# First layer of a hybrid decoder: the RMSNorm root moved from the input to the products

## The chip, the cores and the metric

The kernel runs on one core of one Trainium2 chip. The metric is the device time of one execution in microseconds; the time given for the kernel is the median of three runs. TensorE (PE) multiplies matrices, VectorE (DVE), ScalarE (ACT) and GpSimd (POOL) work on elements, and SyncE (SP) issues the DMAs here.

## The reference

Four layers run over 1040 tokens (16 meta tokens and 1024 of the sequence) of width 1024: sliding-window attention (a), an mLSTM (b), an HGRN2 (c) and attention again. Each layer normalizes the stream, runs its branch and adds the result. What concerns the change is the first attention layer:

```python
def rmsnorm(x, g):
    y = xf * lax.rsqrt(jnp.mean(xf * xf, axis=-1, keepdims=True) + EPS)
    return (y * g.astype(jnp.float32)).astype(x.dtype)
...
q, k, v, z = _split(u @ w_in, (A_W, A_KVW, A_KVW, A_W))
q = rope(rmsnorm(q.reshape(bsz, lp, A_HEADS, A_HD), q_gain), pos)
k = rope(rmsnorm(k.reshape(bsz, lp, A_KV, A_HD), k_gain), pos)
v = v.reshape(bsz, lp, A_KV, A_HD)
o = sliding_window_attention(q, k, v, sinks, valid)
return (o * jax.nn.silu(z.astype(jnp.float32))).astype(u.dtype) @ w_out
```

with `u = rmsnorm(h, norm_gain[i])` in front. The root of the mean square, r, is one number for a token, so (r x g) W = r ((x g) W): it can be applied to the products as well. q and k are normalized once more per head; there r cancels except in the small EPS: with q' = q / r, the root of mean(q'^2) + EPS / r^2 gives the same normalized q.

## The kernel before

Everything is stored with features on the 128 partitions and tokens along the free axis: `x` is 128 x 8 x 1040 fp32. Tokens come in three chunks of 400, 384 and 256 columns (`CHUNKS`). fp32 products are made of three: each operand is split into a high part (a cast to the fp32r type, on ScalarE) and a low part (the remainder, on VectorE; `split`, L194 and L195), and high x high, high x low and low x high add up in PSUM. The normalized input is kept that way in `uh` and `ul`.

`proj` makes one projection tile: 128 output features, for each chunk four steps of two k-slices, six products to a step, 24 to a chunk (L228). `weights` loads a tile's weights in two halves of 256 KB into the `raw` buffers (RAWS = 2) and splits them; a step's third entry, `pre`, does this ahead of time (LOOKAHEAD). An `evac` function takes the finished chunk out of PSUM.

The order of TensorE's work is written by hand: `steps` is a list of [cost, function, pre], and functions such as `later`, `spread` and `weave` insert steps at due times counted in cost. The other engines' instructions, and SyncE's DMAs, are ordered by the Tile scheduler. Each engine runs its own instructions in order. PSUM has eight banks, all shared. Work buffers: `tmp()` gives one of six (TMPS) 128 x 404 buffers, `row()` one of eight 128 x 1040.

The norm (`Norm`) of the first layer runs like this for chunk 0, before any product: square each of eight k-slices on ScalarE (L352), add them in pairs on VectorE (L356), sum over the partitions by a matmul with ones (L364), take Ln and Exp for the root (L338, L339), multiply x by gain and root on VectorE (L386), split the result into `uh` and `ul`. Chunks 1 and 2 follow between the products; their adds are on GpSimd (`squares`, `stat`, `units`, placed by `FIRST`).

The head of layer 0 is three tiles over three chunks: k0, qa and qb (in this order in each chunk; in chunk 0 the first halves of k0 and qa stand together). A q or k chunk is evacuated by ScalarE twice, times the gain (L492) and squared (L493); four small DMAs swap halves for the rotary embedding (L496); later `stat` (k, a matmul with a mask and Ln, Exp) or `stat_q` (q, per token and head, L516 to L519) makes the second norm's root, `rope` rotates, and `k_split` or `q_split` (L444 to L464) splits. Then the attention mixers run, woven step by step with the rest of the projections: v tiles, q tiles, the gate tiles z (`gate_proj`: a sigmoid of five instructions and two products on VectorE, L400 to L412), k1, and the output projections (L322, added to x at L325).

Of the kernel before, what the change touches and what calls it, by code (L numbers as in the profile page):

```python
# [46 lines left out]
PARTS = 4  # L47
FIRST = (0.2, 0.8, 0.85), (0.2, 0.75, 0.8)
# [63 lines left out]
def hybrid_kernel(ctx: ExitStack, tc: tile.TileContext, ins, out, layers=(0, 1, 2, 3)):  # L112
# [47 lines left out]
    eps = cpool.tile([P, 1], F32, name="eps")  # L160
    v.memset(eps, EPS)
    one = cpool.tile([P, 1], F32, name="one")
# [7 lines left out]
    def load_x(n):  # L170
        c0, cn = CHUNKS[n]
        for k in range(KT):
            sp.dma_start(x[:, k, c0 : c0 + cn], ins["xT"][k, :, c0 : c0 + cn])

    load_x(0)
# [35 lines left out]
    def proj(src, evac, chunks=CHUNKS):  # L211
# [129 lines left out]
    class Norm:  # L341
        def __init__(self, i, row=None):
            self.i, self.row, self.acc, self.ps = i, row, {}, {}

        def sq(self, m, n, c0, cn, size=KT):
            if m % size:
                q = tmp()[:, :cn]
            elif self.row is not None and n:
                q = self.row[:, c0 : c0 + cn]
            else:  # L350
                q = (vtile() if n == 2 else tmp())[:, :cn]
            s.activation(q, x[:, m, c0 : c0 + cn], AF.Square)  # L352
            if m % size == 0:
                self.acc[n] = q
            else:
                (v if self.row is None or n == 0 else g).tensor_tensor(self.acc[n], self.acc[n], q, op=ALU.add)  # L356

        def stat(self, n, part=0, parts=1):
            cn = CHUNKS[n][1]

            def fn():
                if part == 0:
                    self.ps[n] = psa()
                pe.matmul(self.ps[n][:, :cn], ones, self.acc[n], start=(part == 0), stop=(part == parts - 1))  # L364
                if part == parts - 1:
                    rstd_from(self.ps[n], self.acc[n], cn, D)

            return [4 * cn * MM, fn, None]

        def squares(self, n, part=0, parts=1):  # L370

            size = KT // parts

            def fn():
                for m in range(part * size, (part + 1) * size):
                    self.sq(m, n, *CHUNKS[n], size)

            return [0.0, fn, None]
# [18 lines left out]

    def sigmoid_from(z, cn):
# [8 lines left out]
    def gate_proj(src, o, chunks=CHUNKS):  # L407
# [6 lines left out]
        return proj(src, evac, chunks)  # L414

    def layer_a(i, j, first, last, fin):
# [69 lines left out]
        def qk_proj(src, gcol, work, fsplit, ch, t=None):  # L486
            late = {}

            def evac(acc, n, c0, cn):
                dst, sq, rot = work(n, c0, cn)  # L490
                late[n] = dst, sq, rot
                s.activation(dst, acc[:, :cn], AF.Identity, scale=R["cons"][:, gcol : gcol + 1])  # L492
                s.activation(sq, acc[:, :cn], AF.Square)  # L493
# [4 lines left out]
            def finish(n, c0, cn):  # L498
                def factors():
# [4 lines left out]
                    late[n] += (R["cs"][1][:, :, c0 - b0 : c0 - b0 + cn],)  # L504

                def stat_q():
# [11 lines left out]
                    s.activation(rq[:, z], st[:, z], AF.Ln, bias=eps, scale=1.0 / 64)  # L518
# [23 lines left out]
            return proj(src, evac, ch), [finish(n, *c) for n, c in enumerate(ch)]  # L542
# [21 lines left out]
        def v_proj(src, jj):  # L564
# [7 lines left out]
            def finish(n, c0, cn):  # L572
                def fn():
# [4 lines left out]
                    for k, b in enumerate(CHUNK_BLOCKS[n]):  # L578
# [7 lines left out]
                        s.copy(parts[:, 0:4:3], src)  # L586
                        v.tensor_tensor(parts[:, 1:3], src, parts[:, 0:4:3].bitcast(F32), op=ALU.subtract)
# [107 lines left out]
        zc = {t: gate_proj(win[12 + t], lambda t=t: R["o", t], chunks) for t in range(8)}  # L695
# [808 lines left out]
```

## Time and profile before

| what | value |
|---|---|
| runs shown | 2623.77, 2625.77, 2625.26 us, median 2625.26 |
| profiled execution, its time | 2624.74 us |
| its span (first to last instruction) | 2623.0 us |
| mean granted TensorE clock | 0.993 |
| VectorE, ScalarE, GpSimd busy | 75%, 64%, 10% of the span |
| DMA | 135.92 MB, mean 52 GB/s |

In a page's groups a line reads: source line, engine, operation, output <- inputs with shapes, count, then busy time and mean ns of one, then the idle time before them and what ended it. A line of the waits reads: who waited, for whom, total us, times, longest. A line of the timeline reads: start, length in us, instruction, count, and in brackets the idle time in front of it. SPq is SyncE's queue, where DMAs are issued; L206 are weight loads.

### The profile page before, as it was taken

The page shows a single profiled execution, that of the slowest core. Times are in us where ns is not written, and L with a number is a line of the kernel's source. Part 1 is how long each engine was busy: PE and PEld are TensorE (multiplying, and loading weights), DVE is VectorE, ACT ScalarE, POOL GpSimd, SP SyncE. Part 2 cuts the span into 40 slices and gives each one's busy share as a digit, 9 for nine tenths or more (in the row PEclk, how much of TensorE's full clock was granted, in tenths as well). Part 3 has the DMA queues.
Part 4 walks back from the last instruction along what each step waited for, and adds up shares of the span by engine and source line. Part 5 has one row for each costly group of instructions (what it writes and reads, how often), then busy time and mean ns, then how long its engine had stood idle before and what let it go on. Part 6 is the DMA issues. An engine that isn't in the chain of part 4 may idle for free. (4 is left out here: it accounts for less than half of the span.)

```text
span 2623.0 us, 54248 instructions
## 1 busy us (share of the span) xinstructions
PE 2565.2 (98%) x20422; PEld 2484.6 (95%) x20422; DVE 1970.6 (75%) x5296; ACT 1665.7 (64%) x4374; POOL 249.8 (10%) x502
## 2 busy tenths in 40 slices
PE   7999999989999999999999999999999999999999
PEld 5999999989999999999999999999999999999999
DVE  6798798784747474747475688989787978887996
ACT  6776767565454545454545657878585857767772
POOL 2221221000000000000000000100000100321330
PEclk9999999999999999999999999999999999999999
DMA  4212111021111111111111101011110112212112
GB/s 129 68 50 84 55 44 48 22 66 49 42 56 41 57 41 56 42 53 45 53 45 49 49 26 50 26 42 34 34 42 30 38 51 86 59 50 84 55 39 79
DMA packets 82583, 135.92 MB, mean 52 GB/s; under 512 B 12033, under 2 KB 35713, under 8 KB 82321
## 3 DMA queue, kind: packets, MB, share of 16 engines
q1 hardware_dynamic: 82320, 132.45, 16.2%
q8 instruction: 161, 2.64, 0.4%
q14 instruction: 102, 0.83, 0.1%
HBM read 117.56 MB, written 4.26 MB: 46 GB/s over the span
## 5 line engine op out<-in xcount | busy, mean ns | idle before, releaser
L228 PE MATMUL pj<-uh,wh 128*128 128x256 f32 (+2 forms) x2688 | 916.4, 341 | 9.6 <-ACT uh L194 9.6
L228 PE MATMUL pj<-ul,wh 128*128 128x256 f32 (+2 forms) x2688 | 867.9, 323 | 2.2 <-DVE ul L195 1.7
L228 PE MATMUL pj<-uh,wl 128*128 128x256 f32 (+2 forms) x2688 | 864.6, 322 | 0.0
L228 PEld LDWEIGHTS pj<-uh,wh 128*128 128x128 f32 x2688 | 510.2, 190 | 26.8 <-ACT uh L194 13.2
L228 PEld LDWEIGHTS pj<-ul,wh 128*128 128x128 f32 x2688 | 510.5, 190 | 11.1 <-DVE ul L195 5.8
L228 PEld LDWEIGHTS pj<-uh,wl 128*128 128x128 f32 x2688 | 510.0, 190 | 0.0
L194 ACT CAST wh<-wr 128x512 fp32r<-128x512 f32 (+1 forms) x338 | 203.2, 613 | 110.9 <-PE pj L322 32.7
L195 DVE TENSOR_TENSOR wl<-wr,wh 128x512 fp32r<-128x512 f32 (+1 forms) x338 | 233.7, 701 | 51.6 <-ACT wh L194 49.3
L325 DVE TENSOR_TENSOR x<-x,pj 128x384 f32<-128x384 f32 (+2 forms) x480 | 234.7, 508 | 35.0 <-PE pj L322 33.7
L322 PE MATMUL pj<-yh,wh 128*128 128x384 f32 (+2 forms) x768 | 253.0, 329 | 8.0 <-DVE x L325 6.2
L322 PE MATMUL pj<-yh,wl 128*128 128x384 f32 (+2 forms) x768 | 245.2, 319 | 0.0
L322 PE MATMUL pj<-yl,wh 128*128 128x384 f32 (+2 forms) x768 | 245.2, 319 | 0.0
L277 PE MATMUL pj<-wh,uh 128*128 128x256 f32 (+1 forms) x768 | 231.9, 302 | 0.0
L277 PE MATMUL pj<-wl,uh 128*128 128x256 f32 (+1 forms) x768 | 216.5, 282 | 0.0
L277 PE MATMUL pj<-wh,ul 128*128 128x256 f32 (+1 forms) x768 | 216.2, 281 | 0.0
L635 POOL TENSOR_TENSOR Sm<-Sm,s 128x512 f32<-128x512 f32 (+2 forms) x136 | 142.1, 1045 | 449.4 <-DVE s L634 434.5
L632 ACT ACTIVATE Sm<-Sm,s 128x257 f32<-128x257 f32 (+2 forms) x272 | 130.9, 482 | 79.5 <-DVE s L629 75.3
L404 ACT ACTIVATE t<-t 128x384 f32<-128x384 f32 (+2 forms) x240 | 117.9, 491 | 87.8 <-DVE t L403 86.0
L403 DVE SCALAR_TENSOR_TENSOR t<-pj,t 128x384 f32<-128x384 f32 (+2 forms) x192 | 98.7, 514 | 80.0 <-ACT t L402 78.1
L322 PEld LDWEIGHTS pj<-yh,wh 128*128 128x128 f32 x768 | 144.2, 188 | 11.7 <-DVE x L325 7.4
L194 ACT CAST yh<-r 128x384 fp32r<-128x384 f32 (+2 forms) x120 | 57.1, 478 | 151.9 <-PE pj L322 139.8
L277 PEld LDWEIGHTS pj<-wh,uh 128*128 128x128 f32 x768 | 144.6, 188 | 2.1
(255 smaller groups left out, 5423.0 us busy)
## 6 DMA issues: line engine op xcount, KB each, us to landing
wr<-in_b_win SPq DMA_DIRECT2D x124, 256.0 KB, 2.8
wr<-in_a_win SPq DMA_DIRECT2D x80, 256.0 KB, 2.9
wr<-in_c_win SPq DMA_DIRECT2D x64, 256.0 KB, 2.8
wr<-in_a_wout SPq DMA_DIRECT2D x32, 256.0 KB, 2.8
wr<-in_b_wout SPq DMA_DIRECT2D x32, 256.0 KB, 2.8
t<-t SPq DMA_DIRECT2D x104, 48.0 KB, 1.9
cs<-in_rope SPq DMA_DIRECT2D x11, 400.0 KB, 3.4
cs<-in_rope SPq DMA_DIRECT2D x11, 384.0 KB, 3.6
```

Source lines behind the costliest of these rows:

```text
L194: s.copy(h, src)
L195: v.tensor_tensor(l, src, h.bitcast(F32), op=ALU.subtract)
L228: pe.matmul(acc[:, :cn], a[:, k, :], b[:, k, c0 : c0 + cn], start=(k == 0 and i == 0), stop=(k == KT - 1 and i == 2))
L277: pe.matmul(acc[:cn, :nc], a[:, k, c0 : c0 + cn], m[:, kk, :], start=(k == 0 and j == 0), stop=(k == KT - 1 and j == 2))
L322: pe.matmul(acc[:, :cn], a[:, k, mc], b, start=(k == 0 and i == 0), stop=(k == 1 and i == 2))
L325: v.tensor_tensor(x[:, m, c0 : c0 + cn], x[:, m, c0 : c0 + cn], acc[:, :cn], op=ALU.add)
L403: v.scalar_tensor_tensor(a[:, :cn], z, 0.0, a[:, :cn], op0=ALU.min, op1=ALU.subtract)
L404: s.activation(a[:, :cn], a[:, :cn], AF.Exp)
L632: s.activation(Sm[:nq, u, : nk + 1], Sm[:nq, u, : nk + 1], AF.Exp, scale=-1.0, bias=st[:nq, u : u + 1], accum_out=den[:nq, u : u + 1])
L635: g.tensor_tensor(Sm[:nq, :, :nk], Sm[:nq, :, :nk], den[:nq].rearrange("p (u c) -> p u c", c=1).to_broadcast([nq, 2, nk]), op=ALU.mult)
```

## The change

In the first layer `uh` and `ul` hold x times the norm's gain, without the root. A new class `Scale` makes the root beside it:

- `unit` makes `uh` with one ScalarE pass from x (the gain as scale) and `ul` with one VectorE pass (x times gain minus `uh`).
- `squares` sums the squares per chunk: ScalarE squares chunks 0 and 1, GpSimd chunk 2, and GpSimd does all adds.
- `sums` makes the root twice: per token on the partitions (`rcol`, and `ecol` = EPS times mean square plus EPS squared) by a product of each block with a column of ones, and along the free axis in `row` by a matmul with ones, Ln and Exp; the row is also written to DRAM.
- `fetch` reads that row back, broadcast to 128 partitions.

The root is applied behind the products: k0's chunks are multiplied by `row`; k1's and the gates' by a fetched row, whose DMA is issued when the second quarter of the chunk's products is (`early`); v's blocks by `rcol` when they are split; q is not multiplied, but its second norm takes `ecol` in place of EPS.

The head's order becomes qa, qb, k0 in each chunk, with the first halves of qa and qb together in chunk 0. qb's work buffers are those of the mixers (`idle`). At the start SyncE is given the gain, the first tile's weights, four slices of x, the second tile's weights, four slices of x, then chunk 1 of x. `Norm` loses what only the first layer used.

```diff
-FIRST = (0.2, 0.8, 0.85), (0.2, 0.75, 0.8)
+FIRST = (0.1, 0.2, 0.9), (1.0, 1.1, 1.9)
+SUMS = 0.8, 1.5, 2.5
...
+                    if part == 1 and early is not None:
+                        early(n, c0, cn)
...
+    class Scale:
...
+        def unit(self, n, k):
...
+            def fn():
+                gain = ngain[:, self.i, k : k + 1]
+                s.activation(uh[:, k, cs], x[:, k, cs], AF.Identity, scale=gain)
+                v.scalar_tensor_tensor(ul[:, k, cs], x[:, k, cs], gain, uh[:, k, cs].bitcast(F32),
+                                       op0=ALU.mult, op1=ALU.subtract)
...
+        def squares(self, n):
...
+                for m in range(KT):
+                    q = tmp()[:, :cn] if m else acc
+                    z = x[:, m, c0 : c0 + cn]
+                    if n < 2:
+                        s.activation(q, z, AF.Square)
+                    else:
+                        g.tensor_tensor(q, z, z, op=ALU.mult)
+                    if m:
+                        g.tensor_tensor(acc, acc, q, op=ALU.add)
...
+        def sums(self, n):
...
+                pc = psa()
+                for k, b in enumerate(bs):
+                    q0 = blk(b)[0] - c0
+                    pe.matmul(pc[:, k : k + 1], acc[:, q0 : q0 + P], ones[:, 0:1], start=True, stop=True)
+                r, e = (z[:, bs[0] : bs[-1] + 1] for z in (self.rcol, self.ecol))
+                s.activation(e, pc[:, : len(bs)], AF.Identity, bias=self.eps2, scale=EPS / D)
+                s.activation(r, pc[:, : len(bs)], AF.Ln, bias=eps, scale=1.0 / D)
+                s.activation(r, r, AF.Exp, scale=-0.5)
+                pr = psa()
+                pe.matmul(pr[:, :cn], ones, acc, start=True, stop=True)
+                rstd_from(pr, acc, cn, D)
+                sp.dma_start(self.dram[c0 : c0 + cn], acc[0:1])
...
+        def fetch(self, dst, c0, cn):
+            sp.dma_start(dst[:, :cn], self.dram[c0 : c0 + cn].partition_broadcast(P))
...
+        def early(n, c0, cn):
+            rs[n] = tmp()
+            scale.fetch(rs[n], c0, cn)
+
         def evac(acc, n, c0, cn):
             cs = slice(c0, c0 + cn)
-            a = sigmoid_from(acc[:, :cn], cn)
-            v.tensor_tensor(a[:, :cn], a[:, :cn], acc[:, :cn], op=ALU.mult)
+            z = acc[:, :cn]
+            if scale is not None:
+                z = rs[n][:, :cn]
+                v.tensor_tensor(z, z, acc[:, :cn], op=ALU.mult)
+            a = sigmoid_from(z, cn)
+            v.tensor_tensor(a[:, :cn], a[:, :cn], z, op=ALU.mult)
             v.tensor_tensor(o()[:, cs], o()[:, cs], a[:, :cn], op=ALU.mult)
...
+                if first and t is None:
+                    v.tensor_tensor(sq, sq if fetched else scale.row[:, c0 : c0 + cn], z, op=ALU.mult)
+                    z = sq
+                s.activation(dst, z, AF.Identity, scale=R["cons"][:, gcol : gcol + 1])
+                s.activation(sq, z, AF.Square)
...
+                        v.scalar_tensor_tensor(rq.rearrange("p (k c) -> p k c", c=2),
+                                               st[:, z].rearrange("p (k c) -> p k c", c=2), 1.0 / 64, e,
+                                               op0=ALU.mult, op1=ALU.add)
+                        s.activation(rq, rq, AF.Ln)
...
+                            s.activation(high, src, AF.Identity, scale=r)
+                            v.scalar_tensor_tensor(parts[:, 1:3], src, r, high.bitcast(F32), op0=ALU.mult, op1=ALU.subtract)
...
+            parts = [tile_of([z[0][n]], [z[1][n]]) for z in ((qa, qb, k0) if first else (k0, qa))]
...
-    for k in range(PARTS):
-        steps += [norm.squares(0, k, PARTS), norm.stat(0, k, PARTS)]
-    steps += [norm.unit(0, k) for k in range(KT)]
+    norm = Scale(layers[0])
+    steps += [norm.unit(0, k) for k in range(KT)] + [norm.squares(0)]
...
+            for n in (2, 1, 0):
+                later(seq, (at(SUMS[n]), norm.sums(n)))
+            for n in (2, 1):
+                t0, t1, t2 = (at(z) for z in FIRST[n - 1])
+                later(seq, *sorted([(t0, norm.squares(n))] + norm.units(n, t1, t2), key=lambda e: e[0]))
...
+    pres = [z for z in steps if z[2] is not None]
+    for z, k0, k1 in ((pres[0], 0, 4), (pres[1], 4, 8)):
+        z[2]()
+        z[2] = None
+        load_x(0, k0, k1)
     load_x(1)
```

More of the change, by code (lines that the diff above doesn't have):

```diff
@@ L693, in mixers @@
             return segs
-        zc = {t: gate_proj(win[12 + t], lambda t=t: R["o", t], chunks) for t in range(8)}
+        zc = {t: gate_proj(win[12 + t], lambda t=t: R["o", t], chunks, scale) for t in range(8)}
         oc = {t: proj_out(wout[t - 1], wout[t], lambda k, t=t: R["o", t - 1 + k], chunks,
@@ L698, in layer_a @@
         kg0, kfin0 = qk_proj(win[0], 1, work_rows(3), k_split(0), CHUNKS)
-        kg1, kfin1 = qk_proj(win[1], 1, tmps, k_split(1), CHUNKS)
+        kg1, kfin1 = qk_proj(win[1], 1, tmps, k_split(1), CHUNKS, fetched=first)
         vg0, vfin0 = v_proj(win[2], 0)
         vg1, vfin1 = v_proj(win[3], 1)
-        qg = {t: qk_proj(win[4 + t], 0, tmps, q_split(t), chunks, t) for t in range(8)}
+        qg = {t: qk_proj(win[4 + t], 0, idle if first and t == 1 else tmps, q_split(t), chunks, t) for t in range(8)}
         def q_pair(p):
@@ L1343, in hybrid_kernel @@
         if i % 3 == 0:
-            head, body, oa, ob = layer_a(i, i // 3, tail is None, i == 3, fin)
+            head, body, oa, ob = layer_a(i, i // 3, tail is None, i == 3, fin, norm if tail is None else None)
         elif i % 3 == 1:
```

135 lines of the change are left out of this document (75 added, 60 removed).

## Prediction

> **What bounds the kernel now.** I read the page's summary first, then the waits of TensorE, then the first 82 us in order of time.
>
> ```profile
> span 2623.0 us, 54248 instructions
> PE 2565.2 (98%) x20422; PEld 2484.6 (95%) x20422; DVE 1970.6 (75%) x5296; ACT 1665.7 (64%) x4374; POOL 249.8 (10%) x502
> PE   7999999989999999999999999999999999999999
> ```
>
> TensorE is busy 98% of the span, and only the first of the 40 slices (65.6 us each) shows a 7. So the question is what the first 82 us lose, and whether anything later loses. TensorE's waits, first in the head (0 to 82 us), then in the rest of the layer up to 450 us:
>
> ```profile
> PE pj L228 <- ACT uh L194: 9.1, 8, 2.9
> ...
> PE pa L364 <- POOL r L356: 2.0, 1, 2.0
> PE pj L228 <- DVE ul L195: 1.7, 4, 0.6
> ```
>
> ```profile
> PE pt L647 <- POOL Sm L635: 2.5, 4, 1.2
> PE pm L621 <- DVE Pl L650: 1.7, 1, 1.7
> PE pt L577 <- ACT t L570: 0.4, 1, 0.4
> ```
>
> In the head every wait is for the normalized input (`uh`, `ul`) or its statistic. Behind the head TensorE waits 4.6 us in three kinds of wait, and 0.5 in two smaller ones, of 369; so there TensorE sets the time, and whatever shortens the head shortens the run by as much.
>
> The start, in order of time:
>
> ```profile
> 0.74 3.71 SPq L173 DMA_DIRECT2D x<-in_xT  x8
> 3.27 1.00 ACT L352 ACTIVATE t<-x 128x400 f32<-128x400 f32 x2 [1.26 <-DMA x<-in_xT]
> 14.06 1.62 ACT L194 CAST uh<-t 128x400 fp32r<-128x400 f32 x3 [0.70 <-DVE t L386]
> 14.64 0.70 PE L228 MATMUL pj<-uh,wh 128*128 128x400 f32 x1 [2.75 <-ACT uh L194]
> ```
>
> The first x lands at 3.27, yet the first product starts at 14.64: squares, sum, root and scaling stand between. How fast products then run, from the stretches of the head (length, TensorE busy and products; granted clock, DMA share, GB/s; the two long stretches without a shape filter):
>
> ```profile
> 14.64:19.92 5.28, 4.96 (x14) 1.00 0.42 142
> 20.17:28.80 8.63, 8.63 (x47) 1.00 0.74 228
> 57.24:60.60 3.36, 3.36 (x18) 1.00 0.24 59
> 78.32:81.35 3.03, 3.03 (x25) 1.00 0.11 30
> 44.00:54.00 10.00, 8.60 (x29) 0.50 0.19 54
> 64.00:78.00 14.00, 12.31 (x47) 0.52 0.16 44
> ```
>
> A product costs 8.63/47 = 0.184 us at 400 columns, 3.36/18 = 0.187 at 384, 3.03/25 = 0.121 at 256. A tile of 24 products per chunk is 24 x 0.492 = 11.8 us, and the head's three tiles (k0, qa, qb) 35.4. The head's last product ends at 81.35. The first stretch runs at 5.28/14 = 0.377 instead of 0.184: 2.7 us lost to a slow start. In 44 to 54 and 64 to 78 the granted clock is 0.50 and 0.52: 10 x 0.50 + 14 x 0.48 = 11.7 us lost.
>
> Small matmuls between them:
>
> ```profile
> 28.80 0.83 PE L525 MATMUL pa<-r,masks 128*128 128x400 f32 x2
> 31.60 0.91 PE L364 MATMUL pa<-r,ones 128*128 128x384 f32 x2 [1.98 <-POOL r L356]
> 33.44 0.95 PE L516 MATMUL pa<-masks,t 128*128 128x2 f32 x8
> 57.00 0.59 PE L364 MATMUL pa<-r,ones 128*128 128x256 f32 x2
> 60.60 0.72 PE L516 MATMUL pa<-masks,t 128*128 128x2 f32 x6
> 82.44 0.50 PE L516 MATMUL pa<-masks,t 128*128 128x2 f32 x4
> ```
>
> k's statistic, about 2.3 for three chunks; q's 2 x (0.95 + 0.72) = 3.3 inside the head; the norm's 1.5 after the start. With the 35.4 that is 42.5. Check: 14.64 + 42.5 + 2.7 + 11.7 + waits after the start (9.1 - 2.75 + 2.0 + 1.7 = 10.1) = 81.6 against 81.35. The head is understood.
>
> **The change part by part.**
>
> *The first product no longer waits for the root.* Only x, ngain, the weights and one ScalarE pass (`uh`) stand before it. SyncE now sends ngain and two weight halves first. At 3.71/8 = 0.46 us an issue, the first x goes out at about 2.1 instead of 0.74.
>
> The rate of transfers in the first 82 us, in slices of 2.05 us:
>
> ```profile
> GB/s 9 261 283 379 375 397 380 367 52 17 306 229 234 164 88 77 33 4 0 4 75 25 0 19 173 43 53 0 67 29 0 0 0 79 21 82 100 18 0 60
> ```
>
> A weight half takes 2.9 us from issue to landing (median of the run):
>
> ```profile
> wr<-in_a_win SPq DMA_DIRECT2D x80, 256.0 KB, 2.9
> ```
>
> From 6 us on 367 to 397 GB/s move, before that 261 to 283. The two halves (524 KB) stand 1.9 us ahead of x at 272: first x at 3.27 + 0.4 for ngain + 1.9 = 5.6, plus a pass of 1.62/3 = 0.54: first product at 6.1 (bounds 5.4 if transfers overlap more, 7.4 if the weight's cast is last). The new pass (a scale read from a column) isn't in the trace; its nearest rows are the square at 3.27 (0.50) and the cast at 14.06 (0.54); I take the cast.
>
> *TensorE's need in the head.* 35.4 for the tiles; k's statistic for two chunks inside the head, 1.6 (k0 now stands last); q's 2 x (0.95 + 0.72 + 0.50) = 4.3; the new `sums` per chunk one full matmul like L364 and one product per block like L516's: (0.91 + 0.95) + (0.9 + 0.72) + (0.59 + 0.50) = 4.5. Sum 45.8. The slow start stays: 2.7.
>
> *The data's pace.* x's first chunk (1.64 MB) and two weight tiles (1.05 MB) take 7.9 us at some 340 GB/s, so all of it is there near 11. Two buffers (RAWS = 2) hold the raw halves of a weight tile, so the second tile's go out only when the first tile's have landed (0.74 + 0.46 + 2.9 = 4.1 for the first half) and are cast and subtracted; if SyncE has issued x's slices meanwhile, they stand behind 1.6 MB. k0's weights come later still: behind x's second chunk it is 4.8 MB in all, 14.1 us + 3.2 = 17.3, plus the cast 17.9, when TensorE wants them at 6.1 + 2.7 + 48 x 0.184 = 17.6. So waits of 0 (weights slip ahead of x) to 7 us (3 at the second tile, 4 at k0 if chunk 2 of x goes first too). I take 2.
>
> *The vector side.* The totals of the first 81.35 us come first below. The old units' multiply by the root goes, 24 instructions; `ul` becomes a multiply and subtract in one. Four adds leave VectorE; the last chunk's squares and all adds are GpSimd's.
>
> ```profile
> sum 81.35, PE 62.56 PEld 52.18 DVE 50.63 ACT 51.22 POOL 13.99; mean PE 12.51 PEld 10.44 DVE 10.13 ACT 10.24 POOL 2.80
> ```
>
> The groups concerned (count, busy and mean ns of one):
>
> ```profile
> L386 DVE SCALAR_TENSOR_TENSOR t<-x,ngain,r 128x384 f32<-128x384 f32 (+1 forms) x16 | 8.4, 546 | 4.3 <-ACT r L339 4.3
> L386 DVE SCALAR_TENSOR_TENSOR t<-x,ngain,t 128x400 f32<-128x400 f32 x8 | 5.4, 720 | 2.2 <-ACT t L339 2.2
> ```
>
> ```profile
> L356 POOL TENSOR_TENSOR r<-r,t 128x384 f32<-128x384 f32 x7 | 7.5, 1069 | 22.8 <-ACT t L352 22.5
> L356 POOL TENSOR_TENSOR r<-r,t 128x256 f32<-128x256 f32 x7 | 5.8, 826 | 17.5 <-ACT t L352 17.0
> ```
>
> VectorE: 50.6 - 13.8 - 2.3 (four adds at 0.57, the price of L464's row below), plus some 3 for k0's row product and q's small sums: 37.5; `ul` lies between that 0.57 and L386's 0.72, so up to 3.4 more. ScalarE: 51.2 less eight squares of 256 columns (0.5 each at 400), plus nine instructions on a few columns: about 50. GpSimd: 7 adds at about 1.1, 7.5, and 15 at 0.826: 27.6, twice what it was. A new head of some 56 us of work has room for VectorE, and ScalarE is 50/56 = 89% full; that will cost some waits. But `uh` and `ul` for chunks 1 and 2 no longer hang on a statistic, so the long waits before `uh`, and with them the half clock, should mostly go. Against 10.1 + 11.7 us before I leave 3.5 (0 to 11).
>
> The head's end: 6.1 + 45.8 + 2.7 + 2 + 3.5 = 60.1, gain 81.35 - 60.1 = 21.2.
>
> *Behind the head.* Each of 24 gate evacuations gets one VectorE product (some 0.55 us, as L464's), 13 us in all, and a 200 KB broadcast fetch on SyncE, issued after the first quarter of its products into a buffer of TMPS; k1's three chunks the same. V's split and q's statistic change form, not count.
>
> ```profile
> 150.00:175.00 25.00, 25.00 (x173) 23.78 (x172) 22.30 (x66) 21.48 (x64) 6.40 (x10) 1.00 0.18 61
> 425.00:450.00 25.00, 25.00 (x162) 24.97 (x161) 18.22 (x36) 16.49 (x37) 0.42 (x1) 1.00 0.28 82
> ```
>
> ```profile
> SPq L206 <- DVE wl L195: 108.8, 27, 25.1
> ```
>
> Where gates run, VectorE is 73 to 89% full and TensorE still does not wait; DMA is at 18 to 28%. So most of the 13 us is covered by TensorE's own products; if that cover were gone it would cost up to 13. In return the bank of PSUM comes free after one instruction instead of six, worth at most the 5.1 us that TensorE waits there. I take a loss of 1.5 (from -3 to +6).
>
> Gain 21.2 - 1.5 = 19.7. The profiled execution took 2624.74, 0.5 below the median 2625.26. Against the median: **2605.6**.
>
> **Two rules that speak against it.** The trace grants 0.50 after a wait of 2.9 us. The Trainium skill ("TensorE: Matmul & The Clock Gate", Part 1, "The HAM clock gate") has the clock fall to half after an idle window of about 3.4 us and come back after one as long of steady work; the trace agrees roughly, with 2.9. By it the waits of the pacing could each drag some 3.4 us at half speed behind them, an estimate of 1.7 us each, 61.8 in place of 60.1.
>
> GpSimd and VectorE disturb each other in the trace:
>
> ```profile
> 24.90 3.31 POOL L356 TENSOR_TENSOR r<-r,t 128x384 f32<-128x384 f32 x3 [3.16 <-ACT t L352]
> 25.11 0.93 DVE L428 TENSOR_SCALAR cons<-cons 128x16 f32<-128x16 f32 x1
> 47.78 0.57 DVE L464 TENSOR_TENSOR qs<-t,qs 64x400 fp32r<-64x400 f32 x1
> 48.58 6.25 POOL L356 TENSOR_TENSOR r<-r,t 128x256 f32<-128x256 f32 x7 [17.03 <-ACT t L352]
> 52.26 1.99 DVE L464 TENSOR_TENSOR qs<-t,qs 64x400 fp32r<-64x400 f32 x2 [3.30 <-ACT qs L463]
> ```
>
> The same subtraction takes 0.57 alone and 1.0 while GpSimd adds; a tiny one takes 0.93. That is the first rival's mechanism. The Trainium skill ("SBUF — State Buffer", "Who interferes with whom") says that a VectorE instruction with two SBUF inputs and a GpSimd one that reads SBUF shut each other out for a whole instruction; the rows agree.
>
> **The rivals.**
>
> *A, VectorE starved by GpSimd.* `ul` is a two-input VectorE instruction and TensorE's second product needs it. With GpSimd busy 27.6 us, some 27 VectorE instructions take 0.4 longer: 11 us, most of it while `ul` of chunks 0 and 1 and the weights' low halves are due. TensorE then waits as before, and half-clock stretches stay. For it: the rows above. Against: VectorE lost 16 us of work. Waits at 11.5 instead of 3.5: gain 11.7, **2613.6**.
>
> *B, slower.* SyncE's queue is in order, and weight loads wait in it for raw buffers: 108.8 us in 27 waits, 4.0 each. A fetch behind one arrives late, the gate's evacuation stands, its PSUM bank stays taken, and TensorE stops. It decides once TensorE loses 21.2/24 = 0.88 us per fetch; at 1.2 us each, 28.8 us go: 2625.3 - 21.2 + 28.8 = **2633**. Against: eight banks, and the fetch has three quarters of a group to arrive.
>
> *C, all stalls gone.* Weights arrive in time and nothing else waits: 6.1 + 45.8 + 2.7 = 54.6, gain 26.7, body even: **2598.5**.
>
> **How the numbers follow.** Forecast 0.60, A 0.19, C 0.13, B 0.08. The forecast's own bounds run from 2600 to 2611; to hold 8 in 10 the range reaches past C's figure and A's: 2597 to 2617. The measurement tells 0.2%, 5.3 us, from no change: A's slow end and B's mild end give 0.04 for no change, B's rest 0.06 for slower, 0.90 for faster.
>
> **What would show it.** First product near 6.1 us; the first vg0 product (now 81.35) near 60; no stretch of ten us at half clock; waits of TensorE for `uh` under 3 us beside short ones for `wh` near 10 and 18. A would show `ul` waits and VectorE instructions of 1.0 us, B waits before gate products or a lengthened 60-to-430 stretch. Wrong would be an unchanged start, or a body longer by over 6 us.

## The result, and the profile after

The changed kernel takes 2635.05 us (median of 8 runs, 2632.55 to 2639.73) against 2626.06 for the kernel before beside it: a ratio on record of 1.0031 with an interval of 1.0020 to 1.0041 (the two medians by themselves give 1.0034). It is slower by 0.3%, where 2605.6 and a gain of 0.75% were forecast. Its profiled execution took 2633.37 with a span of 2631.6, 8.6 us over the span of before.

The page's summary: span, TensorE's busy time, its 40 slices of 65.8 us.

```profile
span 2631.6 us, 54400 instructions
...
PE 2567.6 (98%) x20434; PEld 2492.9 (95%) x20434; DVE 1982.8 (75%) x5323; ACT 1668.8 (63%) x4375; POOL 268.2 (10%) x517
...
PE   7998999989999999999999999999999999999999
```

The first slice still has its 7, and the 8 in the ninth stood there before; new is the 8 in the fourth, 197 to 263 us. The head first. In order of time, TensorE's first product and the first product of the tile vg0 behind the head:

```profile
6.11 0.70 PE L229 MATMUL pj<-uh,wh 128*128 128x400 f32 x1 [6.11 <-ACT uh L398]
...
66.95 0.34 PE L229 MATMUL pj<-uh,wh 128*128 128x400 f32 x1
```

Before, that vg0 product came at 81.35: the head gave 14.4 us. All of it and 8.6 more are lost behind it, 23.0 in all. TensorE's waits in the head (total, times, longest), and two stretches of it (length, then busy time and instructions of PE, PEld, DVE, ACT, POOL; granted clock, DMA share, GB/s):

```profile
PE pj L229 <- ACT uh L398: 6.1, 1, 6.1
PE pj L229 <- ACT wh L193: 4.4, 1, 4.4
PE pa L591 <- ACT t L568: 3.2, 1, 3.2
PE pj L229 <- DVE wl L194: 0.5, 1, 0.5
```

```profile
22.00:28.00 6.00, 5.42 (x15) 4.85 (x16) 6.00 (x6) 4.08 (x9) 5.68 (x5) 0.50 0.38 132
...
33.60:42.00 8.40, 8.35 (x31) 8.33 (x32) 4.12 (x8) 5.44 (x17) 6.26 (x10) 0.50 0.22 55
```

After the start two waits are left, for k0's weights (4.4, and 0.5 for their low half) and for q's statistic (3.2). Behind each the clock is granted at 0.50, for 6 and for 8.4 us, so these two waits cost 8.1 us of standing and (5.42 + 8.35)/2 = 6.9 of half speed.

The waits behind the head, 65 to 450 us:

```profile
PE pa L608 <- ACT t L568: 8.5, 3, 5.0
PE pm L710 <- DVE Pl L739: 4.0, 2, 2.5
PE pt L736 <- POOL Sm L724: 3.6, 4, 1.9
```

The first row is new: L608 is k's statistic, three times, once for each chunk of k1. The kernel before waited 0.2 us in that place. Around it, SyncE's queue, VectorE, ScalarE and TensorE in order of time, from four answers of the timeline:

```profile
238.12 2.42 SPq L571 DMA_DIRECT2D t<-t  x4
240.64 0.53 SPq L446 DMA_DIRECT2D t<-scaled  x1
...
246.44 2.67 SPq L571 DMA_DIRECT2D t<-t  x4
249.21 0.53 SPq L446 DMA_DIRECT2D t<-scaled  x1
...
245.21 0.55 DVE L565 TENSOR_TENSOR t<-t,pj 128x384 f32<-128x384 f32 x1 [4.08 <-DMA t<-scaled]
...
248.62 0.57 DVE L617 TENSOR_TENSOR t<-t,t 128x400 f32<-128x400 f32 x1
...
245.80 0.61 ACT L567 ACTIVATE t<-t,cons 128x384 f32<-128x384 f32 x1 [4.33 <-DVE t L565]
...
239.09 0.94 PE L608 MATMUL pa<-t,masks 128*128 128x400 f32 x2 [2.00 <-ACT t L568]
247.03 0.91 PE L608 MATMUL pa<-t,masks 128*128 128x384 f32 x2 [1.56 <-ACT t L568]
255.07 1.22 PE L608 MATMUL pa<-t,masks 128*128 128x256 f32 x2 [4.95 <-ACT t L568]
```

Read it as a ring. The swaps of one chunk go out at 238.12; only behind them, at 240.64, the fetch of the root for the next chunk; the product with it starts at 245.21, the scaling at 245.80, the statistic at 247.03, the next swaps at 246.44, the next fetch at 249.21. The statistics stand 7.9 and 8.0 us apart, although a chunk's 24 products need 4.4 at most. SyncE stands for 3.8 us before the swaps of 246.44 and hardly at all before the fetch behind them. But the third fetch, at 249.21, goes out just when VectorE's last use of the first chunk's row ends (L617, 248.62 + 0.57 = 249.19); with six work buffers, three to a chunk, this is the buffer that the third chunk's row goes into. From issue to landing, by the list of DMA issues, the fetch is slower than a swap (size of each, median us):

```profile
t<-t SPq DMA_DIRECT2D x36, 50.0 KB, 2.0
t<-scaled SPq DMA_DIRECT2D x9, 200.0 KB, 3.4
t<-scaled SPq DMA_DIRECT2D x9, 192.0 KB, 4.5
```

What the stage lost, in stretches of ten us (columns as above), after and then before:

```profile
240.00:250.00 10.00, 8.44 (x45) 7.76 (x43) 4.94 (x10) 5.19 (x11) 0.00 (x0) 0.83 0.53 148
250.00:260.00 10.00, 5.05 (x15) 4.71 (x15) 4.75 (x9) 5.67 (x12) 0.00 (x0) 0.68 0.51 145
...
sum 40.00, PE 31.43 PEld 29.51 DVE 23.08 ACT 24.55 POOL 1.40; mean PE 7.86 PEld 7.38 DVE 5.77 ACT 6.14 POOL 0.35
```

```profile
sum 40.00, PE 39.33 PEld 37.82 DVE 29.70 ACT 31.30 POOL 4.12; mean PE 9.83 PEld 9.46 DVE 7.43 ACT 7.82 POOL 1.03
```

From 230 to 270 TensorE is busy 7.9 us less than before, and 8.44 x 0.17 + 5.05 x 0.32 = 3.1 us are lost to the clock: 11 us. The ring stands in the one stage where no attention step is woven between a tile's products, so nothing covers it.

### The profile page after: what moved, and what is told of

Read it like the earlier page. It is cut to its first block, busy times and chain, and to the rows that moved or that the text cites. A ratio compares the mean times of both kernels' runs of the same rounds, so it can differ in the third digit from the quotient of the medians.

```text
span 2631.6 us, 54400 instructions
## 1 busy us (share of the span) xinstructions
PE 2567.6 (98%) x20434; PEld 2492.9 (95%) x20434; DVE 1982.8 (75%) x5323; ACT 1668.8 (63%) x4375; POOL 268.2 (10%) x517
## 4 chain that ended last, share of the span: by engine, by line
PE 77%; DVE 11%; ACT 7%; DMA 2%; issue 2%; POOL 1%; SPq 0%; DVEq 0%; ACTq 0%; POOLq 0%
PE pj L229 37%; PE pj L323 15%; PE pj L278 10%; PE po L755 2%; PE pt L736 1%; PE po L998 1%; ACT Sm L721 1%; DVE wl L194 1%; PE pa L1012 1%; PE po L1000 1%; DVE Sm L718 1%; DMA cs<-in_rope 1%; PE pj L274 1%; PE pm L710 1%; PE pm L711 1%
## 5 line engine op out<-in xcount | busy, mean ns | idle before, releaser
L194 DVE TENSOR_TENSOR wl<-wr,wh 128x512 fp32r<-128x512 f32 (+1 forms) x338 | 235.7, 707 | 53.0 <-ACT wh L193 50.3
L721 ACT ACTIVATE Sm<-Sm,s 128x257 f32<-128x257 f32 (+2 forms) x272 | 130.9, 483 | 88.2 <-DVE s L718 84.4
L278 PEld LDWEIGHTS pj<-wl,uh 128*128 128x128 f32 x768 | 144.9, 189 | 1.9
```

The costliest lines, as they stand in the source:

```text
L194: v.tensor_tensor(l, src, h.bitcast(F32), op=ALU.subtract)
L278: pe.matmul(acc[:cn, :nc], a[:, k, c0 : c0 + cn], m[:, kk, :], start=(k == 0 and j == 0), stop=(k == KT - 1 and j == 2))
L721: s.activation(Sm[:nq, u, : nk + 1], Sm[:nq, u, : nk + 1], AF.Exp, scale=-1.0, bias=st[:nq, u : u + 1], accum_out=den[:nq, u : u + 1])
```

## The experiments

Each is an edit of the changed kernel; the ratio is to the kernel before, run beside it. "vg0" is the first product of that tile, the end of the head; "exp 65" and "exp 73" are the starts of the 65th and 73rd exponential of the mixers (L721 in the changed kernel; k1's tile lies between them, and the 73rd is the first of the pair of heads behind it), all from the timeline of the profiled execution, whose span stands last. Kernels whose head is the same as the changed one's (e1 to e7, e11) have vg0 at 66.31 to 67.99, so a difference of a us or so says nothing there.

| kernel | ratio (interval) | vg0 | exp 65 | exp 73 | span |
|---|---|---|---|---|---|
| before | 1 | 81.35 | 223.6 | 272.9 | 2623.0 |
| after | 1.0031 (1.0020 to 1.0041) | 66.95 | 212.1 | 273.5 | 2631.6 |
| e1 k1 plain | 0.9994 (0.9985 to 1.0004) | 67.15 | 213.2 | 263.5 | 2624.6 |
| e2 gates plain | 1.0014 (1.0004 to 1.0023) | 67.60 | 212.5 | 272.5 | 2629.5 |
| e3 both | 0.9965 (0.9952 to 0.9978) | 67.99 | 211.9 | 261.9 | 2616.0 |
| e4 k1's root elsewhere | 0.9999 (0.9990 to 1.0009) | 66.31 | 211.8 | 262.6 | 2620.3 |
| e5 gates' fetch alone | 0.9976 (0.9966 to 0.9987) | 66.68 | 211.9 | 261.7 | 2617.7 |
| e6 gates' product alone | 0.9978 (0.9969 to 0.9988) | 66.71 | 211.2 | 261.2 | 2617.8 |
| e7 gates' root elsewhere | 0.9989 (0.9979 to 0.9998) | 67.39 | 214.8 | 264.8 | 2622.2 |
| e8 squares late | 1.0002 (0.9993 to 1.0012) | 69.20 | 216.2 | 266.8 | 2626.4 |
| e9 squares' own buffers | 0.9995 (0.9986 to 1.0005) | 67.94 | 213.3 | 263.3 | 2623.3 |
| e10 head without root | 0.9986 (0.9976 to 0.9996) | 68.36 | 212.6 | 262.4 | 2621.0 |
| e11 gates' last product on GpSimd | 0.9999 (0.9990 to 1.0009) | 66.61 | 214.1 | 264.1 | 2624.9 |
| e12 e10 and e11 | 0.9987 (0.9978 to 0.9996) | 68.87 | 213.5 | 263.1 | 2618.4 |
| e13 constants early | 0.9968 (0.9956 to 0.9980) | 62.11 | 207.3 | 256.9 | 2617.7 |
| e14 and squares late | 0.9963 (0.9951 to 0.9976) | 60.83 | 206.9 | 257.7 | 2615.7 |
| e15 and sums on VectorE | 0.9947 (0.9932 to 0.9961) | 57.48 | 203.6 | 253.4 | 2613.0 |
| e16 constants early, alone | 0.9978 (0.9968 to 0.9987) | 63.74 | 209.8 | 260.6 | 2623.7 |
| e17 e15, gates' root elsewhere | 0.9948 (0.9933 to 0.9962) | 56.88 | 203.5 | 254.5 | 2614.8 |
| e18 all roots, order of e15 | 0.9991 (0.9981 to 1.0001) | 60.25 | 206.8 | 258.5 | 2619.7 |

### Which part loses behind the head: e1, e2, e3

e1 leaves the root out of k1 (k's norm divides by k's own size, so the root cancels up to EPS), e2 leaves it out of the gates, e3 both.

```diff
-        kg1, kfin1 = qk_proj(win[1], 1, tmps, k_split(1), CHUNKS, fetched=first)
+        kg1, kfin1 = qk_proj(win[1], 1, tmps, k_split(1), CHUNKS, plain=True)
...
-                if first and t is None:
+                if first and t is None and not plain:
...
-        zc = {t: gate_proj(win[12 + t], lambda t=t: R["o", t], chunks, scale) for t in range(8)}
+        zc = {t: gate_proj(win[12 + t], lambda t=t: R["o", t], chunks) for t in range(8)}
```

> k1's chunks are neither multiplied by the root nor wait for a fetch (the root cancels in k's own norm up to EPS); everything else as in the changed kernel. Theory K (the loss is k1's chain of fetch, product, half swaps and next fetch, 12 us between the 70th and 72nd softmax step): the jump goes, the run takes about 2623 us, 12 less than the changed kernel. Rival G (the loss is spread over the gates: 24 products on VectorE, 24 fetches in SyncE's queue, one more of six buffers held): at most 3 us less, 2632 or more.

> The gates take the products without the root (left out: the gate's root), with no fetch and no extra VectorE product; k1 keeps its fetch. Theory K: only the smaller losses of the gate stretches go, 4 to 6 us, about 2630 us. Rival G: 10 to 18 us less, 2617 to 2625.

> Neither k1 nor the gates are multiplied by the root (left out: the gate's root). If the head's gain of 16 us at its end is kept once both are gone, the run takes 2610 to 2613 us. If the body has a cost of its own from starting earlier (vector work pushed out of the head), it takes over 2616.

e1's statistics of k1, in order of time, without a wait:

```profile
237.97 0.83 PE L608 MATMUL pa<-t,masks 128*128 128x400 f32 x2
242.53 0.81 PE L608 MATMUL pa<-t,masks 128*128 128x384 f32 x2
245.36 0.59 PE L608 MATMUL pa<-t,masks 128*128 128x256 f32 x2
```

They stand 4.6 and 2.8 us apart where the changed kernel has 7.9 and 8.0. From exp 65 to exp 73 e1 needs 50.3 us, before 49.3, after 61.4. So k1's three chunks cost 1.0031 - 0.9994 = 0.37%, 9.7 us. The gates' 24 cost 0.17% beside k1's ring (after against e2) and 0.29% without it (e1 against e3), 4.5 to 7.6 us; since the two parts share a stage, they don't add exactly, and the 0.17% is hardly larger than the interval of such a difference.

e3 also came out on the second side of its expectation. With neither root nor fetch behind the head it is 13.4 us ahead of the kernel before at vg0 (81.35 against 67.99) and only 7.0 at the end: 1.7 us are gone by exp 65, 0.7 more by exp 73 and 4.0 behind that. So 6.4 us of the head's gain are lost by something else than the root. Of these, some 1.5 are half clock: e3 and the kernel before both have a wait of TensorE of 8.9 us near 545 us, and with it the clock is granted at 0.50 from 538.6 to 548.9 in e3 (TensorE busy for 5.75 of it), but from 549.1 to 556.0 before (busy for 2.85). The rest isn't attributed by any run.

### Landing, queue or buffer: e4

e4 keeps k1's root and its product; the fetch goes into a buffer of the output projections (tag yh, idle in this stage), and the three work buffers are taken at the evacuation, as before the change.

```diff
-                late[n] = work(n, c0, cn)
-                scale.fetch(late[n][1], c0, cn)
+                late["r", n] = tpool.tile([P, 400], F32R, tag="yh", name=nm("yh"), bufs=YS)[:, :cn].bitcast(F32)
+                scale.fetch(late["r", n], c0, cn)
```

> k1's root is fetched into a buffer of its own (one of the yh buffers, idle there) and not into k1's work buffer, so the fetch needs no free buffer of the six. If the shortage of work buffers puts the fetch behind the swaps of the chunk before, TensorE's waits for k1's statistic go from 8.5 to under 2 us and the run takes about 2624 us. If the landing of 4.0 to 4.5 us alone is the cost, the waits stay above 5 us and the run takes over 2629.

SyncE's issues of the fetches, and TensorE's statistics, in e4:

```profile
186.07 0.33 SPq L446 DMA_DIRECT2D yh<-scaled  x1
193.31 1.04 SPq L446 DMA_DIRECT2D yh<-scaled  x2
...
236.85 0.94 PE L607 MATMUL pa<-t,masks 128*128 128x400 f32 x2
241.51 0.81 PE L607 MATMUL pa<-t,masks 128*128 128x384 f32 x2
246.69 0.70 PE L607 MATMUL pa<-t,masks 128*128 128x256 f32 x2 [2.19 <-ACT t L567]
```

All three fetches are out before 195, some 40 us ahead of use, and the ratio is 0.9999: within its interval the same as e1; from exp 65 to exp 73 e4 needs 50.8 us. So the product and the landing cost next to nothing when the fetch is out early. What costs is that the changed kernel takes three of the six work buffers together with the fetch, which then comes late. e4 takes away both things that hold the fetch in the ring, the buffers of the chunk before and the place behind its swaps in SyncE's queue, and doesn't tell the two apart.

### The gates: e5, e6, e7, e11

On e1's ground, e5 keeps the fetch and its buffer but multiplies one column only; e6 multiplies by a resident tile (`uh`) and fetches nothing; e7 fetches into yh; e11 gives GpSimd the last product of the evacuation. In e5 and e6 the gates lack the root.

```diff
 e5
-                z = rs[n][:, :cn]
-                v.tensor_tensor(z, z, acc[:, :cn], op=ALU.mult)
+                r = rs[n][:, :1]
+                v.tensor_tensor(r, r, acc[:, :1], op=ALU.mult)
 e6
-            rs[n] = tmp()
-            scale.fetch(rs[n], c0, cn)
+            pass
...
+                z = tmp()[:, :cn]
+                v.tensor_tensor(z, uh[:, 0, cs].bitcast(F32), acc[:, :cn], op=ALU.mult)
```

> k1 plain as in e1; the gates keep the fetch of the root into a buffer taken after the first quarter and their evacuation still starts with an instruction that needs it, but that instruction works on one column only, and the gate is taken from PSUM as before (left out: the gates' root, so the output differs). e1 stood at 2625.5 and e3, without root and fetch, at 2617.7: 7.8 us belong to the gates. Theory Q (SyncE's queue and the buffers set the price): all of it stays, 2624 to 2626, with TensorE's waits behind step 104 as in e1. Theory V (VectorE's 24 products of some 0.55 us set it): it goes, 2617 to 2619.

> k1 plain as in e1; the gates are multiplied by a tile that is resident anyway (uh) in place of the root, with no fetch; the buffer is taken at the evacuation (left out: the gates' root and its fetch, so the output differs). Theory Q: 2617 to 2619, as e3. Theory V: 2624 to 2626, as e1. If both this and e5 lie near 2621 the price is shared.

> k1 plain as in e1; the gates' root is fetched into a buffer of the output projections' pool (tag yh, 3 buffers), the product goes into a work buffer taken at the evacuation. All of the result is computed. Theory Q, when the shortage of work buffers is what costs: 2618 to 2621. Theory Q, when the order of SyncE's queue costs: about 2625. Theory V: about 2625.

> k1 plain as in e1; the last product of each of the 24 gate evacuations (o times the gate, both in SBUF) goes from VectorE to GpSimd, so that VectorE has as many of them as before the change. e6 put VectorE's product at some 4 of the gates' 7.7 us. If VectorE's occupation is the price: 2621 to 2622.5. Rival (GpSimd's instructions of 1.1 us slow VectorE's, or delay the softmax products that GpSimd makes): 2625 or more, with longer waits of TensorE for POOL's Sm.

Neither theory holds alone: e5 lies 0.18% under e1 and e6 0.16%, so taking away either the product or the fetch gains. What each costs by itself isn't clear of noise: e5 lies 0.11% above e3 and e6 0.13%, 2.9 and 3.4 us of 7.6 together, with some 0.17% as the interval of such a difference. e7 lies 0.05% under e1, which its interval doesn't separate from nothing. e11 gains nothing; the instruction that leaves VectorE takes 1.16 us on GpSimd instead of 0.59 (400 columns), but TensorE's waits for GpSimd's softmax products stay at 3.6 us, so why the relief of VectorE brings nothing isn't shown. A price of 7.6/24 = 0.3 us a gate is what remains of fetch and product where attention steps are woven between the products. Part of it in e1's trace is half clock: 0.50 is granted from 339.1 to 342.5 and from 410.8 to 414.2, 3.4 us lost, where e3, e5 and e6 have none between 275 and 460. But e9, whose gates are those of e1, has none there either, so this part differs between kernels with the same gates.

### What holds the head: e8 to e10, e13 to e16

The profile names GpSimd as the releaser of q's evacuation (L567) in the changed kernel: its row additions hold work buffers that the evacuation needs. e8 moves the second chunk's squares behind its scaled input; e9 gives the squares six buffers of their own (yh and yl); e10 also leaves the root out of k0 and takes EPS itself in q's statistic, with the sums due later.

```diff
 e8
-FIRST = (0.1, 0.2, 0.9), (1.0, 1.1, 1.9)
+FIRST = (0.95, 0.1, 0.8), (1.0, 1.1, 1.9)
 e9
-                    q = tmp()[:, :cn] if m else acc
+                    q = tpool.tile([P, 400], F32R, tag="yh yl"[3 * (m % 2) :][:2], name=nm("sq"), bufs=YS)[:, :cn].bitcast(F32) if m else acc
 e10, besides
-SUMS = 0.8, 1.5, 2.5
+SUMS = 1.6, 2.2, 2.9
```

> k1 plain as in e1; in the head the squares of the second chunk of x (ScalarE) and their sums (GpSimd) are moved behind that chunk's scaled input, from 0.1 to 0.95 of the first stage. Theory G (GpSimd's 1.2 us adds hold the work buffers, ScalarE's squares wait for these, and behind them stand the cast of k0's weights and q's evacuation): TensorE's waits of 4.4 us for k0's weights and of 3.2 us for q's statistic go to under 1 each, with part of the half clock behind them; the first vg0 product at 54 to 58 instead of some 65, 2615 to 2619. Rival (the transfers set k0's weights): the wait of 4.4 stays over 3, gain 3 at most, 2622 to 2625.

> k1 plain as in e1; in the head the squares of x go into six buffers of the output projections' pool (yh, yl), which nobody uses there, in place of the six work buffers that q's evacuation needs too; their time and order are as in e1. Theory G (GpSimd's slow adds hold the buffers that q's evacuation needs): TensorE's wait of 3.2 us for q's statistic goes to under 1, and no such wait appears at the second chunk, as it did in e8; k0's weights keep a wait of 3 to 5; 2620 to 2623. Rival (the head's waits only move on, since ScalarE's own order sets them): the sum of the head's waits stays within 1 us of e1's 7.7, and so does the time, 2625 to 2626.

> As e9, and in the head k0 takes no root either (it cancels in k's norm up to EPS) and q's statistic takes EPS itself in place of EPS over the root squared, so that nothing in the head waits for the sums, which go from 0.8, 1.5, 2.5 to 1.6, 2.2, 2.9. All of the result is computed, up to EPS. VectorE loses three products of 0.55 us. If the root's place in the head costs (theory G's second half): the first vg0 product at 56 to 60, 2616 to 2620. Rival (k0's weights and VectorE beside GpSimd set the head): within 1 us of e9.

All three miss. e8's wait for k0's weights falls to 2.7 us, but 2.5 for their low half come in place of 0.5; q's wait falls to 1.7, but 2.2 and 1.8 come at the second chunk; the head ends 2 us later than in e1. e9 frees the buffers, and the wait for q's statistic is 2.9 instead of 3.2. In e10, where nothing in the head needs the root any more, it is 4.8. So GpSimd was the releaser that the profile named, and not what held the evacuation. e10's timeline shows that, VectorE and ScalarE in order of time:

```profile
24.81 7.58 DVE L399 SCALAR_TENSOR_TENSOR ul<-x,ngain,uh 128x384 fp32r<-128x384 f32 x7
32.32 0.14 DVE L487 TENSOR_SCALAR cons<-cons 128x1 f32<-128x1 f32 x1
32.38 0.63 DVE L488 TENSOR_SCALAR cons<-cons 128x16 f32<-128x16 f32 x1
...
32.54 0.59 ACT L567 ACTIVATE t<-pj,cons 128x400 f32<-128x400 f32 x1 [5.36 <-issue]
```

q's evacuation scales by a column of `cons`, VectorE prepares that column in an instruction of 0.14 us, and this instruction stands behind seven `ul` of 7.58/7 = 1.08 us, beside GpSimd's additions and squares. The constants arrive from SyncE behind x's second chunk, so they get behind its `ul` too. The changed kernel has the same order, GpSimd, VectorE and ScalarE:

```profile
31.02 1.03 POOL L420 TENSOR_TENSOR r<-r,t 128x256 f32<-128x256 f32 x1
...
32.39 0.14 DVE L487 TENSOR_SCALAR cons<-cons 128x1 f32<-128x1 f32 x1
...
32.62 0.59 ACT L567 ACTIVATE t<-pj,cons 128x400 f32<-128x400 f32 x1 [1.47 <-POOL r L420]
```

The addition that is named ends at 32.05, the scaling of the column at 32.53, and the evacuation starts at 32.62. e13 is e10 with the constants sent ahead of that chunk; e16 is e1 with this edit alone; e14 adds e8's edit to e13; e15, on top of e14, gives VectorE the sums of the first two chunks.

```diff
 e13, e16
-        head[0].insert(0, [0.0, enter, None])
+        head[0].insert(0, [0.0, (lambda: None) if first else enter, enter if first else None])
...
-    for z, k0, k1 in ((pres[0], 0, 4), (pres[1], 4, 8)):
+    for z, k0, k1 in ((pres[1], 0, 4), (pres[2], 4, 8)):
...
+    pres[0][2]()
+    pres[0][2] = None
     load_x(1)
 e15, besides
-                        g.tensor_tensor(acc, acc, q, op=ALU.add)
+                        (v if n < 2 else g).tensor_tensor(acc, acc, q, op=ALU.add)
```

> As e10, and the layer's constants (masks, cons) are sent ahead of the second chunk of x, so that VectorE's two small scalings of cons need not stand behind the scaled inputs of that chunk. In e10's trace q's evacuation (ScalarE, scaled by a column of cons) starts at 32.54, just after VectorE's scalings at 32.32 and 32.38, which stand behind seven ul instructions of 1.08 us beside GpSimd's adds. Theory D (that queue on VectorE, stretched by GpSimd, holds q's evacuation): TensorE's wait of 4.8 us for q's statistic goes to under 1 and part of the half clock with it, the first vg0 product 5 to 8 earlier, 2615 to 2619. Rival (GpSimd and the buffers alone, theory G): the wait stays over 3 and the time within 1 us of e10's 2622.9.

> As e13, and the squares of the second chunk of x come behind its scaled inputs (0.95 in place of 0.1), as in e8. Then ScalarE's cast of k0's weights does not stand behind squares that wait for GpSimd: TensorE's wait of 4.0 for k0's weights to 2 or 3 (e8 had 2.7), another 1 to 3 us less than e13. Rival: the wait moves to VectorE's low halves of the weights (2.5 in e8), no gain over e13.

> As e14, and the sums of squares of the first two chunks are VectorE's (0.56 each) in place of GpSimd's (1.2 each). If GpSimd's disturbance is the price (VectorE's ul at 1.0 instead of 0.64): ul at some 0.64 before 30 us, at or below e14. If VectorE's own load is: 2 to 5 us over e14.

> k1 plain as in e1 and the constants ahead of the second chunk of x, nothing else: the other half of the pair with e9 (squares in their own buffers, constants late: no gain). If both the buffers and the constants hold q's evacuation, as the traces suggest (e1's evacuation waited last for GpSimd's add at 32.89, the constants came at 32.73): within 1.5 us of e1's 2625.5, the wait for q's statistic still over 2. If the constants alone do: 2619 to 2622, wait under 1.

In e13 VectorE's scaling, then q's evacuation on ScalarE:

```profile
15.05 0.14 DVE L487 TENSOR_SCALAR cons<-cons 128x1 f32<-128x1 f32 x1
...
23.21 0.59 ACT L567 ACTIVATE t<-pj,cons 128x400 f32<-128x400 f32 x1
```

The evacuation starts at 23.21 instead of 32.54, the wait for q's statistic is gone, and vg0 starts 6.2 us earlier than in e10. e16 gains 3.4 us of head over e1 and 0.16% of time with that edit alone, the wait for q's statistic gone there too; so the constants held it by themselves, and the joint cause that I had expected from the traces of e1 is refuted. e15, VectorE, GpSimd and TensorE:

```profile
18.00 2.20 DVE L399 SCALAR_TENSOR_TENSOR ul<-x,ngain,uh 128x384 fp32r<-128x384 f32 x4
...
22.76 5.22 DVE L399 SCALAR_TENSOR_TENSOR ul<-x,ngain,uh 128x384 fp32r<-128x384 f32 x6
...
20.66 0.61 POOL L418 TENSOR_TENSOR r<-x 128x256 f32<-128x256 f32 x1 [19.61 <-DMA x<-in_xT]
...
57.48 0.35 PE L229 MATMUL pj<-uh,wh 128*128 128x400 f32 x1
```

The same `ul` takes 2.20/4 = 0.55 us while GpSimd rests. The row at 22.76 puts two of 384 columns and four of 256 together; the two of 384 take 0.95 us each (22.76 to 24.66), beside GpSimd's squares and additions of the third chunk, which run from 20.66. Seven additions more on VectorE a chunk, and the head is 3.4 us shorter than in e14: what GpSimd did there cost more than what it took over.

### Together: e12, e17, e18

e12 is e10 with e11's edit: 0.9987, as e10 (0.9986). e17 is e15 with e7's, and no faster than e15. e18 keeps every root of the change (k1's fetched as in e4) and takes only e15's order of the head.

> e10 and e11 together. If the head's stalls and the gates' price add: the sum of both gains over e1's 2625.5, 2612 to 2617, faster than before by some 0.4 to 0.6%. If a gain of the head is given back behind it (as before, where GpSimd has work from both): 2620 or more.

> As e15, and the gates' root is fetched into the output projections' buffers, as in e7. e7 gained some 1 us over e1: 2612 to 2615. If those buffers are what out1's steps wait for (e7's trace had a wait of 2.6 us of TensorE's mixers): 2615 or more.

> The change with its arithmetic whole: k0, k1, q and the gates take the root as the change has it, with k1's fetched as in e4 (buffers of the output projections), and only the order and place of the head's side work as in e15 (squares into those buffers and behind the second chunk's scaled input, sums of the first two chunks on VectorE, constants early; the sums' due times as in the change). If the head is set by the queues alone (theory D), the place of the root costs next to nothing: head within 2 us of e15's, and 2615 to 2619. Rival (the root in the head costs by itself, as e10's gain over e9 of 3 us would have it): 2619 to 2623.

```profile
60.25 0.34 PE L229 MATMUL pj<-uh,wh 128*128 128x400 f32 x1
```

e18's head ends at 60.25, 2.8 behind e15's; its median doesn't differ from before's. Its profiled execution was the shortest of its ten runs, 4.0 us under the median, so the trace shows less loss than the runs have, and the 0.44% between e15 and e18, the price of the roots of k0, q and k1 and of the earlier sums together, isn't divided further. e15 and e17, in which only V and the gates take the root, lie furthest below the kernel before: e15 by 0.53% with an interval of 0.39 to 0.68, e17 by 0.52%.

## Why the prediction was wrong

*The first product, forecast 6.1: 6.11.* Right, with its working.

*The head's end, forecast 60.1: 66.95.* TensorE's need (45.8), the start and the slow start are 54.6 in the forecast. Without the waits and the half clock the head would have ended at 66.95 - 8.1 - 6.9 = 52.0, so the need was put some 2.6 too high. (e15 says nearly the same: 57.48, less waits of 2.5 and 0.5 and 1.7 of half clock, is 52.8.) The terms that failed are pacing and stalls, 2 + 3.5, which measured 8.1 of waits and 6.9 of half clock. k0's weights were forecast as a matter of transfers. Their two waits, 4.4 and 0.5, are 2.5 and 0.5 in e15, so some 1.9 go away with the order of the squares, the place of the additions and the early constants together; moving the squares alone gained nothing in sum (2.7 and 2.5 in e8). The wait for q's statistic had no term at all: the forecast counted VectorE's load in the head (37.5 of 56, where 45.1 of 66.95 were measured) and not what stands in its queue ahead of a small instruction that others wait for. Rival A had the mechanism, VectorE's two-input instructions slowed beside GpSimd (1.08 against 0.55), but TensorE never waits for `ul` in the head, as A had it. That A's 11.5 us of waits put the head's end at 68.1, near the measured one, is partly luck, since the need was too high.

*Behind the head, forecast a loss of 1.5 (from -3 to +6): 23.0.* This is the step that failed. By the table the gain on before is 14.4 at vg0, 11.5 at exp 65, -0.6 at exp 73 and -8.6 at the end: 2.9 go before k1, 12.1 in k1's stage, 8.0 behind it. "k1's three chunks the same" was the wrong sentence, at 9.7 us by e1: the fetch was costed as covered from VectorE's and DMA's shares in 150 to 175 and 425 to 450, where attention steps stand between the products, and k1's stage, 230 to 270, isn't in the working. There the fetch, the swaps and the buffers close a ring of 8 us around 4.4 us of products. The gates' price, 4.5 to 7.6 us, was the forecast's own upper end (+6) and not its middle. What is left of the 23.0, 5.7 to 8.8 us, falls on the premise "whatever shortens the head shortens the run by as much": e3, without k1's fetch and the gates', loses 6.4 of its 13.4 us.

*Rival B* was the one with a chance of 0.08 that ended on the right side, and its 2633 lies near 2635.05. That is luck in the main. It had SyncE's fetch as the late piece and 0.88 us a fetch as the point of decision, but its place was wrong: not the PSUM bank of a gate but k1's evacuation, whose fetch came late for the sake of buffers and swaps. k1's three fetches lose over 3 us each, the gates' 24 only 0.3 where B's figure takes 1.2.

*Left open:* 1.0 to 2.3 us more are lost on before between 665 and 1530 us, in layers b and later, by the changed kernel (1.3) and all variants (the 97th and the 241st addition to x: 7.2 and 8.4 behind before in the changed kernel, 14.8 and 13.3 ahead in e15), at a granted clock of 1.00 and without a wait of TensorE in the changed kernel. e15 loses 3.1 more from there to its last addition and e1 2.7, e3 nothing and the changed kernel 0.3. Nothing was run on either.

## What to carry to other kernels

Cost a fetch that feeds an evacuation in the stage with the least work woven around it, and write down which buffers it holds from its issue on: buffers taken early from the same few that the chunk before still holds can close a ring, and the ring's period sets the time. Before reading a releaser as the cause, list every input of the waiting instruction, the constants too: the one named here had ended 0.5 us before the constant was ready, and freeing its buffers moved nothing. And before carrying a gain at the head over to the whole run, measure how much of it is left at the end. Sending work from a half-full VectorE to an idle GpSimd can lengthen both where their instructions overlap.

## What the hardware showed unexpectedly

The half clock outlasts the wait: 6.3 us after the wait of 4.4 (22.06 to 28.36), 8.4 after 3.2 (33.66 to 42.01). By the trace's record of the granted clock it begins inside the wait, at 21.53 and at 31.77, and lasts 6.83 and 10.24 us, two and three times 3.41. Every stretch of half clock inside the traces of this case is one, two, three or four times as long as that, so the price of a wait beyond its own length comes in steps of up to 1.7 us. The Trainium skill ("TensorE: Matmul & The Clock Gate", Part 1, "The HAM clock gate") has full speed back after some 3.4 us of steady work. Here it comes 4.8 us after the last pause in the first stretch (23.61 to 28.36). In the second it comes 4.9 us after the first product (37.09 to 42.01), ahead of which stand sixteen small matmuls of two columns. A wait of 3.2 us here costs 7.4 in all, 3.2 and half of 8.4.

The fetch of one row to 128 partitions lands 3.4 to 4.5 us after its issue in chunks of 200 and 192 KB, against 2.0 for a swap of 50 KB.

VectorE's instruction with two SBUF inputs (`ul`, 384 columns) takes 1.08 us beside GpSimd's additions and squares and 0.55 alone. GpSimd's additions of 384 columns get longer too, in e10 from 0.99 us (19.3 to 21.4, VectorE at rest) to 1.30 (21.5 to 28.2). The Trainium skill ("SBUF — State Buffer", "Who interferes with whom") says that such a VectorE instruction contends with a GpSimd one that reads SBUF for ports that one of them holds alone; the trace agrees, and e15 shows what it is worth here, 3.4 us of head for 14 additions moved back.
